# Gate operands laid out in pairs of tokens, and five of layer 0's eight output weight blocks loaded beside the last steps of the recurrence

## The chip, the cores and the metric

The kernel runs on one core of a Trainium2 chip. A core has five engines that run side by side, each through its own instructions in order: TensorE (PE, matmuls; its weight loads are listed apart as PEld), VectorE (DVE), ScalarE (ACT), GpSimd (POOL) and SyncE (SP), which mostly issues DMAs. The metric is the device time of one launch in microseconds.

## The reference

The reference is a trunk of two layers over 256 context tokens and 512 latent tokens of width 1024. Each layer has a mixer and a feed-forward part, both inside a residual with adaLN modulation:

```python
mix, mix_c = mixer(h, hc, *mix_p, need_ctx=not last)
x = x + g1 * mix
x = x + g2 * peer_ffn(rms_norm(x, norm2) * (1.0 + sc2) + sh2, *peer_p)
```

The mixer of layer 0 is a recurrence (RWKV-7 heads, in both directions) beside a two-dimensional Fourier transform; both are joined and multiplied by `w_out`, a matrix of 1024x1024. The mixer of layer 1 is attention beside a convolution. The feed-forward part looks up experts: for each token and each of 8 heads, 16 of 128x128 experts are chosen by top-k, and only their rows of `pu` and `pv` count:

```python
expert = e1 * N_KEYS + e2
gate = jax.nn.softmax(score, axis=-1)
act = jax.nn.gelu(jnp.einsum("thkd,td->thk", pu[expert], tc).astype(jnp.float32),
                  approximate=False) * gate
return jnp.einsum("thk,thkd->td", act.astype(pv.dtype), pv[expert])
```

## The kernel before, in words

Tokens are worked on in tiles of 128: two tiles of context and four of latent tokens. Matrices are split into a high and a low part in a reduced float32 type, and each product is made of three matmuls (high by high, high by low, low by high).

The feed-forward part has two ways of computing the same thing. For some tiles (the two context tiles in layer 0, one latent tile in layer 1) the chosen rows are **gathered**: GpSimd issues an indirect DMA for one chosen row of each token (line 1128, 128 such steps per tile for `pu` and 128 for `pv`), and VectorE multiplies and sums it (line 1133) or adds it, scaled (line 1142). For the other tiles (four in layer 0, three in layer 1) it is **dense**: all 16384 experts are computed for every token (`up_part`, whose matmuls are line 391 with the output `pS`), then multiplied with a gate matrix that is zero for experts that were not chosen, and multiplied with `pv` (lines 1287 and 1316, output `acc`).

`dense_gates` makes that gate matrix, 128x128 for each token. The 128 choices of a token lie on the partitions. For four tokens at a time VectorE makes one-hot rows of both index halves, `o` (line 1106, compares the iota `iob` with the indices `gxe`), and multiplies one of them with the gate values in a high and a low part, `og` (line 1108, `gxg`). Then, for each of the four tokens, two matmuls (line 1114) contract over the 128 choices: the weights are the 128 one-hot columns of the token, the streamed operand its 128 gated columns. ScalarE evicts four tokens at once (line 1116, two instructions) into `gbig`. Since VectorE writes `o` and `og` with the four tokens innermost, a matmul reads its 128 columns with a step of four float16 elements, 8 bytes.

The mixer of layer 0 (`mixer0`) runs its recurrence in 12 steps (`rwkv_step`). The context tiles are done first, and their feed-forward part runs beside steps 4 to 11. After the recurrence `out_norm` multiplies the latent tiles with `w_out` in the order 3, 4, 2, 5 (line 985, matmuls with the output `po`, 48 per tile). `out_k` (from line 941) loads the eight row blocks of `w_out`: each block in two halves of 512 columns into the buffer `woraw` (line 948), then split: ScalarE casts the high part `wohi` (line 378), GpSimd subtracts for the low part `wolo` (line 381). In the kernel before, `out_w` loads all eight blocks, with three `woraw` buffers (`WL[0]`), inside the front of layer 0's dense part, which stands in a block of raised priority.

The order of instructions on each engine is set by a list scheduler when the program is built. It follows the order in the code, except where a part stands under `tc.high_priority(n)`, which moves it ahead. So the order is fixed before the run, and each engine works through its own list, waiting at semaphores.

Of the kernel before, what the change touches and what calls it, by code (L numbers as in the profile page):

```python
# [8 lines left out]
F32 = mybir.dt.float32  # L9
F32R = mybir.dt.float32r  # L10
BF16 = mybir.dt.bfloat16
F16 = mybir.dt.float16
# [3 lines left out]
OP = mybir.AluOpType  # L16
# [14 lines left out]
CQ = 3  # L31
FB = 2
GSC = 32768.0
GW = 4
GQ = 0
NO = 0
NK = 0
WI = 9
WL = [3, 2]
HF = 300  # L40
OL = [[0, 1, 2, 3], []]
# [25 lines left out]
OB = 4  # L67
# [126 lines left out]
class Net:  # L194
# [26 lines left out]
    def setup(self, st):  # L221
# [22 lines left out]
        self.ka1 = ka  # L244
        self.iob = p.tile([128, 128, GW], F16, name="iob")
        nc.vector.tensor_copy(self.iob, self.k("iota")[:, :, None].to_broadcast([128, 128, GW]))
        self.io16 = p.tile([128, 16, 16], BF16, name="io16")
# [204 lines left out]
    def mixer0(self, st, early, xin, xout, xend):  # L452

        tc = self.tc
        with ExitStack() as s1:
            self.mixer0_in(s1, xin)
            with ExitStack() as s2:
# [24 lines left out]
                for i in range(4, NCH):  # L482
                    with tc.high_priority(HP):
                        self.rwkv_step(i)
                    if i == WI and NO + NK == 0:
                        wo = []
                    elif i == WI:
                        wk = self.tp(early, "ow", 1, side="right")
                        wo = self.out_k(wk, 0, range(NK))
                        oe = {t: wk.tile([128, 8, 128], F32, name=f"od{t}") for t in (2, 3, 4, 5)[4 - NO:]}  # L490
# [596 lines left out]
    def dense_gates(self, e1, e2, gate, gd, sp, gp, pp, pt):  # L1087

        nc = self.nc
        V = nc.vector  # L1090


        ee, gg = sp.tile([128, 2, 128], F16, name="gxe"), sp.tile([128, 2, 128], F16, name="gxg")
        for dst, x, sc in ((ee[:, 0], e1, 1.0), (ee[:, 1], e2, 1.0), (gg[:, 0], gate, GSC)):
            p = pt.tile([128, 128], F32, name="gtp")
            nc.tensor.transpose(p, x.rearrange("p a b -> p (a b)"), self.k("ident"))
            nc.scalar.mul(out=dst, in_=p, mul=sc)
        V.scalar_tensor_tensor(out=gg[:, 1], in0=p, scalar=GSC, in1=gg[:, 0], op0=OP.mult, op1=OP.subtract)
        W, H = GW, 64
        for h0 in range(0, 128, H):  # L1100
            gh = [gp.tile([128, 64, H], F32, name="gbig") for _ in range(2)]
            for t0 in range(h0, h0 + H, W):
                w = slice(t0, t0 + W)
                o = sp.tile([128, 2, 128, W], F16, name="o12", bufs=OB)
                og = sp.tile([128, 2, 128, W], F16, name="og", bufs=OB)
                V.tensor_tensor(out=o, in0=self.iob[:, None].to_broadcast([128, 2, 128, W]),  # L1106
                                in1=ee[:, :, None, w].to_broadcast([128, 2, 128, W]), op=OP.is_equal)
                V.tensor_tensor(out=og, in0=o[:, 0:1].to_broadcast([128, 2, 128, W]),  # L1108
                                in1=gg[:, :, None, w].to_broadcast([128, 2, 128, W]), op=OP.mult)
                for k0 in range(0, W, 4):  # L1110
                    p = pp.tile([128, 4, 128], F32, name="gps")
                    for j in range(4):
                        for i in range(2):
                            nc.tensor.matmul(p[:, j, :], o[:, 1, :, k0 + j], og[:, i, :, k0 + j], start=(i == 0), stop=(i == 1))  # L1114
                    for i, g in enumerate(gh):
                        nc.scalar.mul(out=g[:, :, t0 - h0 + k0:t0 - h0 + k0 + 4].rearrange("p e t -> p t e"), in_=p[:, :, i * 64:i * 64 + 64],  # L1116
                                      mul=1.0 / GSC)
            for i, g in enumerate(gh):
                nc.scalar.dma_start(gd[h0 // H, :, i * 64:i * 64 + 64, :], g)

# [500 lines left out]
```

## Time and profile before

| | us |
|---|---|
| median of 3 runs | 4701.33 (4699.65 to 4709.9) |
| the profiled execution | 4686.23 |
| its span, first to last instruction | 4684.4 |
| PE busy | 4278.9 (91%) |
| weight loads of PE busy | 3540.5 (76%) |
| VectorE busy | 3552.1 (76%) |
| ScalarE busy | 1739.0 (37%) |
| GpSimd busy | 1577.4 (34%) |

The mean granted clock of TensorE is 0.95 of full speed (2.4 GHz). Matmuls are pipelined: one starts while the one before it still drains, and its end in the profile is modelled. So the duration of a matmul in the profile is no price; the distance from start to start in an unbroken run is. In the profile's rows a type `f32` on PE can be the reduced type, since both have four bytes; line 391, 985, 1287 and 1316 use the reduced type, lines 558 and 1014 plain float32.

### The profile page before, as it was taken

To read this page: it belongs to the slowest core of one execution; us is meant where nothing else is said; L and a number is where in the kernel's file an instruction comes from. 1 tells how busy PE (TensorE), PEld (TensorE's weight loads), DVE (VectorE), ACT (ScalarE), POOL (GpSimd) and SP (SyncE) were. 2 spreads that over 40 slices of the span, in tenths; PEclk is the share of its full clock that TensorE was granted. 3 is DMA by queue.
4 is the path that set the end of the run, shared out by engine and by line. 5 is a ranking of instruction groups with operands and counts; after the bars stand their busy time and mean duration, and the time that the engine had idled before them with its cause. 6 is when DMAs were issued, how large, how long until landed. Compare 5 with 4: busy or idle time off the path is not lost. (4 is left out here: it accounts for less than half of the span.)

```text
span 4684.4 us, 69766 instructions
## 1 busy us (share of the span) xinstructions
PE 4278.9 (91%) x26113; PEld 3540.5 (76%) x26113; DVE 3552.1 (76%) x6647; ACT 1739.0 (37%) x2845; POOL 1577.4 (34%) x1146
## 2 busy tenths in 40 slices
PE   7998899985769999999999999879999989999998
PEld 5775567874647887877777888666789978888887
DVE  2776566689899887888788787695488877788885
ACT  3443123333224556222222222336436643333333
POOL 1332112214643120444444344383220024444440
PEclk9998898997889999999999999889999989999999
DMA  4444873335777767989888888410135589999994
GB/s 167 97 105 106 268 272 115 111 127 184 225 240 266 250 242 263 321 303 322 292 306 314 302 307 286 154 31 32 70 110 183 201 326 330 337 350 334 335 332 153
DMA packets 487278, 1061.99 MB, mean 227 GB/s; under 512 B 95094, under 2 KB 265846, under 8 KB 477206
## 3 DMA queue, kind: packets, MB, share of 16 engines
q1 hardware_dynamic: 371740, 594.02, 38.5%
q0 software_dynamic: 110592, 402.70, 24.6%
q10 hardware_dynamic: 4608, 60.82, 3.3%
q8 instruction: 205, 3.36, 0.3%
q14 instruction: 133, 1.09, 0.1%
HBM read 927.83 MB, written 129.56 MB: 226 GB/s over the span
## 5 line engine op out<-in xcount | busy, mean ns | idle before, releaser
L1128 POOL DMA_INDIRECT row<-in_l_pv_dram,gi x384 | 539.0, 1404 | 912.1 <-DVE rows L1142 778.1
L1128 POOL DMA_INDIRECT row<-in_l_pur_dram,gi x384 | 477.5, 1243 | 972.2 <-DVE ga L1133 511.7
L391 PE MATMUL pS<-h2hi,whi 128*128 128x512 f32 (+1 forms) x2048 | 754.6, 368 | 36.9 <-ACT a L1233 32.2
L391 PE MATMUL pS<-h2hi,wlo 128*128 128x512 f32 (+1 forms) x2048 | 752.7, 368 | 5.1 <-DVE wlo L381 5.1
L391 PE MATMUL pS<-h2lo,whi 128*128 128x512 f32 (+1 forms) x2048 | 751.8, 367 | 0.0
L1133 DVE CUSTOM_DVE_ANT_0 row<-row,rows 128x1024 f32<-128x1024 f32 x384 | 495.7, 1297 | 170.5 <-DMA row<-in_l_pur_dram,gi 168.1
L378 ACT CAST whi<-wraw 128x1024 fp32r<-128x1024 f32 x327 | 343.9, 1053 | 750.5 <-PE pS L391 571.6
L1142 DVE SCALAR_TENSOR_TENSOR rows<-row,ga,rows 128x1024 f32<-128x1024 f32 x381 | 488.2, 1281 | 158.5 <-DMA row<-in_l_pv_dram,gi 156.4
L1287 PE MATMUL acc<-vhi,ahi 128*128 128x512 f32 x1536 | 469.6, 392 | 11.3 <-ACT ahi L378 11.3
L1287 PE MATMUL acc<-vlo,ahi 128*128 128x512 f32 x1536 | 478.3, 391 | 0.0
L1287 PE MATMUL acc<-vhi,alo 128*128 128x512 f32 x1536 | 472.1, 391 | 3.5 <-DVE alo L381 3.5
L391 PEld LDWEIGHTS pS<-h2hi,whi 128*128 128x128 f32 x2048 | 390.3, 191 | 84.6 <-ACT a L1233 34.1
L391 PEld LDWEIGHTS pS<-h2hi,wlo 128*128 128x128 f32 x2048 | 389.3, 190 | 47.8 <-DVE wlo L381 6.8
L391 PEld LDWEIGHTS pS<-h2lo,whi 128*128 128x128 f32 x2048 | 390.5, 191 | 44.0
L381 DVE TENSOR_TENSOR wlo<-wraw,whi 128x1024 fp32r<-128x1024 f32 x266 | 325.6, 1224 | 85.6 <-ACT whi L378 84.8
L378 ACT CAST vhi<-vraw 128x1024 fp32r<-128x1024 f32 x256 | 265.0, 1050 | 215.3 <-PE acc L1287 107.7
L381 DVE TENSOR_TENSOR vlo<-vraw,vhi 128x1024 fp32r<-128x1024 f32 x256 | 309.8, 1221 | 40.1 <-ACT vhi L378 39.9
L1287 PEld LDWEIGHTS acc<-vhi,alo 128*128 128x128 f32 x1536 | 289.0, 188 | 66.3 <-DVE alo L381 5.1
L1287 PEld LDWEIGHTS acc<-vhi,ahi 128*128 128x128 f32 x1536 | 288.1, 189 | 65.9 <-ACT ahi L378 11.9
L1287 PEld LDWEIGHTS acc<-vlo,ahi 128*128 128x128 f32 x1536 | 289.3, 188 | 61.3
L378 ACT CAST ahi<-a32f 128x384 fp32r<-128x384 f32 (+1 forms) x148 | 83.3, 563 | 594.6 <-DVE a32f L1303 279.5
L1116 ACT ACTIVATE gbig<-gps 128x256 f32<-128x256 f32 x448 | 235.5, 661 | 156.8 <-PE gps L1114 144.4
(460 smaller groups left out, 8175.9 us busy)
## 6 DMA issues: line engine op xcount, KB each, us to landing
wraw<-in_l_pu_dram SPq DMA_DIRECT2D x256, 512.0 KB
vraw<-in_l_pv_dram SPq DMA_DIRECT2D x256, 512.0 KB
gd<-gbig ACTq DMA_DIRECT2D x28, 2048.0 KB
mw<-in_l_mod_w_dram SPq DMA_DIRECT2D x48, 1024.0 KB
gt<-gd SPq DMA_DIRECT2D x64, 512.0 KB
wraw<-in_l_pq_dram SPq DMA_DIRECT2D x48, 512.0 KB
gt<-gd SPq DMA_DIRECT2D x64, 384.0 KB
ab<-arb SPq DMA_DIRECT2D x24, 768.0 KB
```

What stands on the lines that cost most here:

```text
L378: e.copy(out=hi, in_=src)
L381: return (e_lo or nc.vector).tensor_tensor(out=lo, in0=src, in1=hi.bitcast(F32), op=OP.subtract)
L391: nc.tensor.matmul(ps, a[:, k, :], b[:, k, t0:t0 + n], start=s, stop=e)
L1116: nc.scalar.mul(out=g[:, :, t0 - h0 + k0:t0 - h0 + k0 + 4].rearrange("p e t -> p t e"), in_=p[:, :, i * 64:i * 64 + 64], mul=1.0 / GSC)
L1128: nc.gpsimd.indirect_dma_start(out=r, out_offset=None, in_=self.I[f"l{l}_{src}"], in_offset=bass.IndirectOffsetOnAxis(ap=idx[:, s:s + 1], ...
L1133: V.tensor_tensor_reduce(out=r, in0=r, in1=acc, scale=1.0, scalar=0.0, op0=OP.mult, op1=OP.add, accum_out=act[:, s:s + 1])
L1142: V.scalar_tensor_tensor(out=acc, in0=r, scalar=act[:, s:s + 1], in1=acc, op0=OP.mult, op1=OP.add)
L1287: nc.tensor.matmul(acc[t][h2], x[:, q], y[:, h2 * 512:(h2 + 1) * 512], start=s, stop=z)
```

## The change

In `dense_gates` the operands are laid out in pairs of tokens (`GW` 2): a group of four tokens is two pairs, and within a pair the two tokens are innermost. A matmul now reads its columns with a step of two float16 elements, 4 bytes. VectorE still has two instructions for four tokens, each of 1024 elements; the matmuls and the evictions are as many as before, of the same shapes. The small tiles `gxe` and `gxg` are laid out in pairs as well, and the iota has 256 columns in place of 512.

In `mixer0`, after step 8 of the recurrence in the code (`WI` 8), `out_k` is called for row blocks 0 to 4 (`NK` 5) with two `woraw` buffers, outside any raised priority; `out_w` then loads blocks 5 to 7.

```diff
-GW = 4
+GW = 2
-NK = 0
-WI = 9
+NK = 5
+WI = 8
...
-        ee, gg = sp.tile([128, 2, 128], F16, name="gxe"), sp.tile([128, 2, 128], F16, name="gxg")
-        for dst, x, sc in ((ee[:, 0], e1, 1.0), (ee[:, 1], e2, 1.0), (gg[:, 0], gate, GSC)):
+        W, H = GW, 64
+        two = lambda x: x.rearrange("p (a b) -> p a b", b=W)
+        ee, gg = sp.tile([128, 64, 2, W], F16, name="gxe"), sp.tile([128, 64, 2, W], F16, name="gxg")
+        for dst, x, sc in ((ee[:, :, 0], e1, 1.0), (ee[:, :, 1], e2, 1.0), (gg[:, :, 0], gate, GSC)):
...
-            for t0 in range(h0, h0 + H, W):
-                w = slice(t0, t0 + W)
-                o = sp.tile([128, 2, 128, W], F16, name="o12", bufs=OB)
-                og = sp.tile([128, 2, 128, W], F16, name="og", bufs=OB)
...
+            for t0 in range(h0, h0 + H, 4):
+
+                w = slice(t0 // W, t0 // W + 2)
+                o = sp.tile([128, 2, 2, 128, W], F16, name="o12", bufs=OB)
+                og = sp.tile([128, 2, 2, 128, W], F16, name="og", bufs=OB)
+                B4, B5 = [128, 4, 128, W], [128, 2, 2, 128, W]
...
+                V.tensor_tensor(out=og, in0=o[:, :, 0:1].to_broadcast(B5), in1=gg[:, w, :, None].to_broadcast(B5), op=OP.mult)
+                p = pp.tile([128, 4, 128], F32, name="gps")
+                for j in range(4):
+                    a, b = divmod(j, W)
+                    for i in range(2):
+                        nc.tensor.matmul(p[:, j, :], o[:, a, 1, :, b], og[:, a, i, :, b], start=(i == 0), stop=(i == 1))
```

Line numbers in `dense_gates` and `gather` shift by two to three: the row gather is line 1130 after, its multiply line 1135.

The first place where the order moves is GpSimd (POOL) around the output projection of layer 0. `wolo` of block 0 to 7 is numbered 11404, 11414 and so on to 11474 before; after, blocks 0 to 4 are 9860 to 9900, blocks 5 to 7 are 11457 to 11477. `row` is the buffer of a gathered row. Before:

```order
L894 TENSOR_TENSOR hy<-hy,hm 128x768 x2
L381 TENSOR_TENSOR wolo_11404<-woraw,wohi_11403 128x512 x2
L381 TENSOR_TENSOR wolo_11414<-woraw,wohi_11413 128x512 x2
L381 TENSOR_TENSOR wolo_11424<-woraw,wohi_11423 128x512 x2
L381 TENSOR_TENSOR wolo_11434<-woraw,wohi_11433 128x512 x2
L381 TENSOR_TENSOR wolo_11444<-woraw,wohi_11443 128x512 x2
L381 TENSOR_TENSOR wolo_11454<-woraw,wohi_11453 128x512 x2
L1128 DMA row<-in_l_pur_dram,gi_7653 128x1024 x3
L381 TENSOR_TENSOR wolo_11464<-woraw,wohi_11463 128x512 x2
L381 TENSOR_TENSOR wolo_11474<-woraw,wohi_11473 128x512
L1128 DMA row<-in_l_pur_dram,gi_7653 128x1024
L381 TENSOR_TENSOR wolo_11474<-woraw,wohi_11473 128x512
```

After, at the same place:

```order
L381 TENSOR_TENSOR wolo_11457<-woraw,wohi_11456 128x512 x2
L381 TENSOR_TENSOR wolo_11467<-woraw,wohi_11466 128x512 x2
L381 TENSOR_TENSOR wolo_11477<-woraw,wohi_11476 128x512 x2
L894 TENSOR_TENSOR hy<-hy,hm 128x768 x2
L1130 DMA row<-in_l_pur_dram,gi_7653 128x1024 x15
L381 TENSOR_TENSOR wolo_9860<-woraw,wohi_9859 128x512
L1130 DMA row<-in_l_pur_dram,gi_7653 128x1024
L381 TENSOR_TENSOR wolo_9860<-woraw,wohi_9859 128x512
L1130 DMA row<-in_l_pur_dram,gi_7653 128x1024 x2
L381 TENSOR_TENSOR wolo_9870<-woraw,wohi_9869 128x512
L1130 DMA row<-in_l_pur_dram,gi_7653 128x1024
L381 TENSOR_TENSOR wolo_9870<-woraw,wohi_9869 128x512
```

Blocks 5 to 7 now stand ahead of the recurrence's last multiply (`hy`), and blocks 0 to 4 behind it and behind 15 gathers; each further half is followed by one or two gathers, so that 28 stand ahead of the last half of block 4.

The second place is SyncE (SP), which issues the loads: `hsq` and `ot` belong to the end of the recurrence, `wraw` and `sk` to the feed-forward part of the context. Before:

```order
L206 DMA hsq<-yd_121 128x768 x2
L206 DMA sk<-in_l_sk_dram 128x128
L206 DMA wraw<-in_l_pq_dram 128x1024
L206 DMA sk<-in_l_sk_dram 128x128
L206 DMA gr_11401<-modd_84 128x1024
L948 DMA woraw<-in_l_w_out_dram 128x512 x3
L206 DMA ot<-od_7763 128x1024
L206 DMA ox<-in_x_dram 128x1024 x2
L948 DMA woraw<-in_l_w_out_dram 128x512 x3
L206 DMA ot<-od_7764 128x1024
L948 DMA woraw<-in_l_w_out_dram 128x512 x10
```

After:

```order
L206 DMA gr_11454<-modd_84 128x1024
L948 DMA woraw<-in_l_w_out_dram 128x512 x3
L206 DMA hsq<-yd_121 128x768 x2
L206 DMA sk<-in_l_sk_dram 128x128
L206 DMA wraw<-in_l_pq_dram 128x1024
L948 DMA woraw<-in_l_w_out_dram 128x512 x3
L206 DMA sk<-in_l_sk_dram 128x128
L206 DMA ot<-od_7763 128x1024
L206 DMA ox<-in_x_dram 128x1024 x2
L206 DMA ot<-od_7764 128x1024
L948 DMA woraw<-in_l_w_out_dram 128x512 x10
```

The six halves of blocks 5 to 7 have moved up, ahead of `hsq` and `ot`; the ten halves of blocks 0 to 4 stand where the last ten stood. The third place is PE at the start of the projection; after:

```order
L909 MATMUL sm<-xg,g_3801 128x128 x3
L985 MATMUL po<-wohi_9859,oh 128x512 x4
L985 MATMUL po<-wolo_9860,oh 128x512
L985 MATMUL po<-wohi_9859,ol 128x512
L985 MATMUL po<-wolo_9860,oh 128x512 x2
L985 MATMUL po<-wohi_9859,ol 128x512
L985 MATMUL po<-wolo_9860,oh 128x512
L985 MATMUL po<-wohi_9869,oh 128x512 x2
```

As before, the projection begins with block 0; the blocks that are ready first, 5 to 7, are the last that a tile needs.

## Rows read from the trace of the kernel before

**Rows 1.** The page: span, busy time, PE in tenths of 40 slices.

```profile
span 4684.4 us, 69766 instructions
...
PE 4278.9 (91%) x26113; PEld 3540.5 (76%) x26113; DVE 3552.1 (76%) x6647; ACT 1739.0 (37%) x2845; POOL 1577.4 (34%) x1146
...
PE   7998899985769999999999999879999989999998
```

**Rows 2.** All engines in three stretches; columns: window, length, busy time (instructions), clock, DMA.

```profile
core 0: us, PE busy (x) PEld busy (x) DVE busy (x) ACT busy (x) POOL busy (x), PEclk, DMA share, GB/s
1488.00:1810.00 322.00, 322.00 (x1797) 270.87 (x1797) 271.28 (x511) 182.49 (x303) 56.11 (x40) 1.00 0.69 244
1810.00:1900.00 90.00, 80.59 (x449) 66.25 (x447) 66.42 (x90) 51.08 (x87) 17.69 (x10) 0.89 0.76 279
3494.00:3790.00 296.00, 288.33 (x1895) 276.85 (x1894) 250.59 (x570) 192.20 (x317) 5.99 (x5) 0.98 0.55 200
```

**Rows 3.** Line 1114: duration min/median/max in ns, and who waited for it.

```profile
L1114 PEld LDWEIGHTS <-o x1792: 111/117/138, 1488.1 to 3789.5; 128*128 128x128 f16 x200
L1114 PE MATMUL gps<-og,o x1792: 273/297/303, 1488.1 to 3789.6; 128*128 128x128 f16 x200
...
  DVE o L1106: 52.3, 66
```

**Rows 4.** Line 1114 alone in the two gate stretches.

```profile
1488.00:1810.00 322.00, 103.23 (x792) 85.82 (x792) 1.00 0.69 244
3494.00:3790.00 296.00, 100.95 (x768) 82.86 (x768) 0.98 0.55 200
```

**Rows 5.** Timeline of PE: start, duration, line, operands, shape, count.

```profile
1488.12 2.98 PE L1114 MATMUL gps<-og,o 128*128 128x128 f16 x24
...
1491.41 0.39 PE L391 MATMUL pS<-h2hi,wlo 128*128 128x512 f32 x1
1491.64 0.39 PE L391 MATMUL pS<-h2hi,whi 128*128 128x512 f32 x1
```

**Rows 6.** Timeline of PE in the projection: 256 columns streamed.

```profile
130.58 0.28 PE L391 MATMUL pjc<-h0hi,whi 128*128 128x256 f32 x1
...
131.53 0.28 PE L391 MATMUL pjc<-h0hi,wlo 128*128 128x256 f32 x1
```

**Rows 7.** Timeline of PE: float32 products with 2 columns streamed.

```profile
432.80 0.70 PE L558 MATMUL pg<-kt,ib 128*128 128x2 f32 x5
```

**Rows 8.** Timeline of PE: float32 products with 128 columns streamed.

```profile
1212.84 1.06 PE L1014 MATMUL psc<-sk,q 128*128 128x128 f32 x8
```

**Rows 9.** Line 558: durations.

```profile
L558 PE MATMUL pg<-kt,ib x72: 165/251/251, 120.5 to 433.2; 128*128 128x2 f32 x72
```

**Rows 10.** Groups of VectorE: busy us, mean ns, idle before and its releasers.

```profile
L381 DVE TENSOR_TENSOR wlo<-wraw,whi 128x1024 fp32r<-128x1024 f32 x266 | 325.6, 1224 | 85.6 <-ACT whi L378 84.8
...
L1106 DVE TENSOR_TENSOR o<-iob,gxe 128x1024 f16<-128x1024 f16 x224 | 151.9, 687 | 54.0 <-PE gps L1114 52.3 <-issue 0.7 <-ACT gxe L1097 0.3
L1108 DVE TENSOR_TENSOR og<-o,gxg 128x1024 f16<-128x1024 f16 x224 | 148.1, 683 | 0.1
```

**Rows 11.** All engines from the output projection to the first gate.

```profile
1100.00:1490.00 390.00, 279.63 (x1200) 222.78 (x1199) 346.87 (x1040) 95.18 (x139) 197.86 (x153) 0.85 0.76 245
```

**Rows 12.** Groups of VectorE from 1000 to 1490 us.

```profile
L1133 DVE CUSTOM_DVE_ANT_0 row<-row,rows 128x1024 f32<-128x1024 f32 x122 | 177.0, 1456 | 38.8 <-DMA row<-in_l_pur_dram,gi 38.6
```

**Rows 13.** Timeline of POOL around the output projection.

```profile
1103.42 1.15 POOL L1128 DMA_INDIRECT row<-in_l_pur_dram,gi  x1 [2.71 <-DVE tci L1027]
...
1118.70 1.42 POOL L381 TENSOR_TENSOR wolo<-woraw,wohi 128x512 fp32r<-128x512 f32 x1
...
1148.03 1.15 POOL L1128 DMA_INDIRECT row<-in_l_pur_dram,gi  x1 [2.92 <-DVE ga L1133]
```

**Rows 14.** Line 985, the output projection, in two stretches.

```profile
1083.00:1148.00 65.00, 33.16 (x96) 20.79 (x95) 0.71 0.54 175
1148.00:1184.00 36.00, 22.18 (x88) 17.44 (x87) 0.93 0.72 240
```

More of the change, by code (lines that the diff above doesn't have):

```diff
@@ L1095, in dense_gates @@
             p = pt.tile([128, 128], F32, name="gtp")
             nc.tensor.transpose(p, x.rearrange("p a b -> p (a b)"), self.k("ident"))
-            nc.scalar.mul(out=dst, in_=p, mul=sc)
-        V.scalar_tensor_tensor(out=gg[:, 1], in0=p, scalar=GSC, in1=gg[:, 0], op0=OP.mult, op1=OP.subtract)
-        W, H = GW, 64
+            nc.scalar.mul(out=dst, in_=two(p), mul=sc)
+        V.scalar_tensor_tensor(out=gg[:, :, 1], in0=two(p), scalar=GSC, in1=gg[:, :, 0], op0=OP.mult, op1=OP.subtract)
         for h0 in range(0, 128, H):
@@ L1101, in dense_gates @@
             gh = [gp.tile([128, 64, H], F32, name="gbig") for _ in range(2)]
-            for t0 in range(h0, h0 + H, W):
-                w = slice(t0, t0 + W)
-                o = sp.tile([128, 2, 128, W], F16, name="o12", bufs=OB)
-                og = sp.tile([128, 2, 128, W], F16, name="og", bufs=OB)
[L1106 to L1117, printed above, removed]
@@ new lines, in dense_gates @@
+            for t0 in range(h0, h0 + H, 4):
[3 more added lines that the diff above has]
+                B4, B5 = [128, 4, 128, W], [128, 2, 2, 128, W]
+                V.tensor_tensor(out=o.rearrange("p a h e b -> p (a h) e b"), in0=self.iob[:, None].to_broadcast(B4),
+                                in1=ee[:, w].rearrange("p a h b -> p (a h) b")[:, :, None].to_broadcast(B4), op=OP.is_equal)
+                V.tensor_tensor(out=og, in0=o[:, :, 0:1].to_broadcast(B5), in1=gg[:, w, :, None].to_broadcast(B5), op=OP.mult)
[4 more added lines that the diff above has]
+                        nc.tensor.matmul(p[:, j, :], o[:, a, 1, :, b], og[:, a, i, :, b], start=(i == 0), stop=(i == 1))
+                for i, g in enumerate(gh):
+                    nc.scalar.mul(out=g[:, :, t0 - h0:t0 - h0 + 4].rearrange("p e t -> p t e"), in_=p[:, :, i * 64:i * 64 + 64],
+                                  mul=1.0 / GSC)
```

## The prediction

> **What bounds the kernel now.** I read the page first: TensorE (PE) is busy for 4278.9 of 4684.4 us, and in its row of slices it is at 9 in slices 15 to 28 and again from slice 32 on [rows 1]. A microsecond taken from PE can therefore be a microsecond of the run, where no other engine is close behind. Next I cut out the stretches in which the gates are built. From 1488 to 1810 us (layer 0) PE is busy for all of 322 us at clock 1.00, VectorE (DVE) for 271.28; from 3494 to 3790 us (layer 1) PE for 288.33 of 296 us, DVE for 250.59 [rows 2]. So PE sets the time there, and DVE stands some 45 to 50 us behind it. VectorE even waits 52.3 us for line 1114 to hand back an operand buffer [rows 3]. ScalarE (182.49 and 192.20 us) and the transfers (0.69 and 0.55 of the DMA engines) are not near a limit [rows 2].
>
> Of what PE does there I took line 1114 by itself: 792 of its 1792 matmuls lie in the first stretch, 768 in the second [rows 4], and 232 more between 1810 and 1900 us (1024 for layer 0's four tiles of 256). The busy time that rows 4 give (103.23 us) is not its price, as the ends of overlapped matmuls are modelled. The price is the distance between starts: 24 of them take 2.98 us, the last 0.297 of it [rows 3, 5], so (2.98 - 0.297) / 23 = 0.117 us each, 1792 x 0.117 = 210 us of PE.
>
> **Part one, the operands' step.** Each of these matmuls loads 128 columns of weights and streams 128 columns, both float16, and takes its columns out of a tile in which neighbours are 4 tokens apart, 8 bytes. After the change they are 2 tokens apart, 4 bytes. What would it cost then? The trace has no float16 matmul with a 4-byte step, so I bound it by rows of 4-byte elements that lie side by side. Neighbouring starts of a 512-column matmul are 0.23 us apart (1491.41, 1491.64) [rows 5]; eight intervals of 256 columns take 131.53 - 130.58 = 0.95 us, 0.119 each [rows 6]. That is 256 / 2.4 = 107 ns of streaming at one column per cycle, and 12 ns beside it. The gate matmul of 128 columns costs as much as one of 256: its step of 8 bytes fits a column every second cycle. By the same line 128 columns at full rate cost 53 + 12 = 65 ns. Eight float32 products of 128 columns take 1.06 us, 0.112 each if the last takes 0.28 [rows 8]; that is 2 x 128 / 2.4 and 5 ns, so two passes over the columns, 0.056 for one. So the lower bound is 0.056, the upper 0.117 (no gain; a dearer one nothing suggests, as the array does the same work). I take 0.065, as its row is the nearest in kind: one pass. Saving: 53 ns per matmul, 42 us in the first stretch, 12 between 1810 and 1900, 41 in the second.
>
> The Trainium skill ("TensorE: Matmul & The Clock Gate", section "Back-to-back issue gap") gives 81 ns for a sustained pair of weight load and matmul at 128 columns; an estimate by that page's figure would be a saving of 36 ns, 28 + 8 + 28 us. No run here shows an 81.
>
> Not all of it can be kept. In the first stretch PE falls to 322 - 42 = 280 us while DVE keeps 271; in the second to 247.6 while DVE keeps 250.6 [rows 2]. DVE does as many instructions on as many elements as before. Two engines so even, coupled through a few buffers, lose some: I take 36 of 42, 30 of 41 and, where PE is busy only 80.59 of 90 us [rows 2], 4 of 12. Sum: 70 us. What follows (the up and down products) keeps PE at 9 and more [rows 1], so it starts earlier and ends earlier by that much.
>
> For DVE the same layout has a price that the trace does not show: the broadcast operand of lines 1106 and 1108 has runs of 2 elements, 4 bytes, where it had 4. Bounds: 0.68 us for 1024 elements as now, or 1.22 us, the price of 1024 float32 elements [rows 10]; below 0.68 it cannot go by the layout, as the count of elements is the same. I take 0.68, since the row is of the same operation and type and the innermost run is still longer than one. The casts that fill the small tiles in pairs (three per token tile) and the iota of half the size are a few instructions of 128 columns per tile, under 1 us together in either direction.
>
> **Part two, the output weights.** The order shows that five blocks are not early. They are not raised in priority, and the three blocks of out_w are; SyncE issues the three first, and blocks 0 to 4 come last, through two raw buffers in place of three. POOL's splits of them stand behind 15 row gathers, and the last behind 28; in the kernel before 4 stood ahead of the last split. The projection needs block 0 first, so it waits. Queued behind POOL's splits are the gathers, behind PE's first projection matmul the other three row tiles and the h2 norms.
>
> Price: the first gather starts at 1103.42 us, the last split at 1118.70; 15 gathers start in the 44.6 us up to 1148.03, 3.2 us each [rows 13]. After, 28 of them stand ahead of the last split: at 3.2 us it ends near 1103 + 90 = 1193, and at the 1.456 us that DVE needs for one [rows 12] near 1103 + 41 + 10 splits of 1.4 = 1158. So the last split is 40 to 74 us late. PE then has all but the first matmuls of 192 left: at 0.23 us 44 us. The projection's end moves from 1184 [rows 14] to 1202 to 1237, 18 to 53 us later. That is covered: DVE sets the pace from 1100 to 1490 us, with 346.87 of 390 us busy, PE 279.63 [rows 11], and the gathers' multiplies that it does in the meantime are ones it would do anyway (244 before the first gate in both orders). What is not covered is DVE's waiting for gathered rows, now 38.6 us for 122 [rows 12], as it has less else to do: I take 5 us, between -15 (rows waited for less later on) and +40 (most of the delay is uncovered).
>
> **Sum.** -70 + 5 = -65 us: 4686.23 profiled (1.83 of it around the span) becomes 4621. The median of the runs is 15.1 us above the profiled one, so 4701.33 - 65 = 4636 us.
>
> **Rivals.**
> - *The pair stays at 0.117.* A weight load with 128 columns would then set the distance, not the step. For it: 5 float32 products that load 128 columns and stream only 2 take 0.70 us, the last 0.251, thus 0.112 each [rows 7, 9], close to 0.117; if their load is one pass, a load costs what a gate pair costs. Against it: if it is two passes, as their streaming is, a load is 0.056, and the pair of rows 8 at the same 0.112 says the same of both. The time: 4701 + 5 = 4706, with part two's ends 4686 to 4741. Chance 0.18. A rule that leads here too: the Trainium skill ("SBUF — State Buffer", section "Door 1: The DMA port swizzle (why `[64,N]` ≈ `[32,N]`)") has lines of 16 bytes and full bandwidth from two hits per line, and a step of 8 bytes already has two. By that rule the step is free now; rows 5 and 6, where 128 columns cost like 256, rather speak against it, without settling it.
> - *A part comes back.* The gain is there, but DVE and the hand-offs keep half of part one, or the late projection is uncovered: -35 + 5 = -30 at half, or -70 + 40 = -30. For it: DVE's 250.59 us against PE's remaining 247.6. Against: the 52.3 us for which DVE waits for PE now. 4671 us, chance 0.20.
> - *Slower: VectorE falls to one element per cycle.* Place: lines 1106 and 1108, 448 instructions, +0.54 us each. In the first stretch 198 of them lie beside the 792 matmuls (two for every 8): DVE 271 + 107 = 378 us against 322, in the second 192: 251 + 104 = 355 against 296, and 58 in the 90 us: +31 on 66.42, 8 over. It would cost 56 + 59 + 8 + 5 = 128 us: 4829. It decides once an instruction costs over (322 - 271) / 198 = 0.26 us more than 0.68; below that PE's gain covers it. Chance 0.05.
>
> **How the numbers follow.** Forecast 0.57, with a range of its own of 4606 to 4666; the three rivals 0.18, 0.20, 0.05. At the low end the whole saving (95 us) and -15 from part two give 4591, at the high end the first rival with 15 us from part two 4716; I take 4592 to 4716. Within 0.2% (9.4 us, about what can be told from no change): 0.10 of the first rival, 0.03 of the second, 0.13 in all. Faster: 0.57 + 0.15 + 0.02 = 0.74. Slower: 0.05 + 0.02 + 0.06 = 0.13.
>
> **What would show it.** Runs of gate matmuls at about 0.065 us between starts; PE below 100% in the gate stretches and VectorE above 90%, its instructions still at 0.68 us, and its wait for line 1114 mostly gone; the first gate matmul within 10 us of 1488; the last split of wolo between 1158 and 1193 us. Wrong it would be by gate matmuls still at 0.117, by VectorE at 1.2 us per instruction, or by a first gate that comes 20 us late.

## The result and the profile after

The changed kernel takes 4651.28 us (median of 4 runs, 4637.62 to 4672.79), the kernel before 4700.49 in the runs beside it: a ratio of 0.9899, with a 95% interval of 0.9857 to 0.9941. That is 49 us less, where 65 were forecast. Its profiled execution takes 4651.99 us.

The page has PE at 4192.2 us, 87 less than before [rows 1], and the span only 34 us shorter (the profiled execution before, 4686.23 us, lay 14 us below the median of its kernel):

```profile
span 4650.2 us, 69814 instructions
...
PE 4192.2 (90%) x26113; PEld 3453.7 (74%) x26113; DVE 3539.1 (76%) x6647; ACT 1732.4 (37%) x2845; POOL 1610.3 (35%) x1146
...
PE   7998899982677999989999999888999989999998
```

A run of gate matmuls on PE (start, duration, line, operands, count) and the line's durations in ns, with the wait of VectorE for it:

```profile
1503.17 1.55 PE L1116 MATMUL gps<-og,o 128*128 128x128 f16 x24
```

```profile
L1116 PEld LDWEIGHTS <-o x1792: 96/97/146, 1503.2 to 3757.7; 128*128 128x128 f16 x200
L1116 PE MATMUL gps<-og,o x1792: 217/218/308, 1503.2 to 3757.8; 128*128 128x128 f16 x200
...
  DVE o L1109: 12.2, 13
```

(1.55 - 0.218) / 23 = 0.058 us from start to start, against 0.117 [rows 3, 5]: at these distances 1792 x 0.059 = 106 us of PE are gone. VectorE's wait for operand buffers falls from 52.3 us to 12.2. All engines over the gate stretches of both layers, from the first gate matmul to the last (window, length, busy time of PE, weight loads, VectorE, ScalarE, GpSimd, then clock and DMA share), before and then after, and VectorE's two instructions (busy us, mean ns):

```profile
1488.00:1850.00 362.00, 355.40 (x2043) 298.81 (x2043) 304.95 (x565) 215.33 (x366) 56.11 (x40) 0.97 0.67 239
3532.00:3790.00 258.00, 251.65 (x1684) 240.55 (x1683) 213.92 (x451) 169.65 (x289) 5.99 (x5) 0.97 0.56 206
```

```profile
1503.00:1831.00 328.00, 328.00 (x2189) 268.80 (x2187) 303.94 (x558) 218.56 (x373) 74.65 (x40) 1.00 0.75 272
3531.00:3758.00 227.00, 212.15 (x1679) 201.46 (x1677) 209.69 (x450) 166.07 (x286) 7.66 (x6) 0.97 0.65 235
```

```profile
L1111 DVE TENSOR_TENSOR og<-o,gxg 128x1024 f16<-128x1024 f16 x224 | 147.6, 686 | 0.1
L1109 DVE TENSOR_TENSOR o<-iob,gxe 128x1024 f16<-128x1024 f16 x224 | 147.4, 686 | 13.4 <-PE gps L1116 12.2 <-ACT gxe L1099 0.7
```

Layer 0's gates now lie within 328 us and layer 1's within 227, where the matmuls' first and last starts were 361 and 257 us apart before. In layer 0 PE is now busy for all of 328.00 us. VectorE's price is unchanged at 686 ns [rows 10].

Around the output projection the trace has GpSimd's first gather, first late split and last split:

```profile
1104.11 1.14 POOL L1130 DMA_INDIRECT row<-in_l_pur_dram,gi  x1 [39.59 <-DVE tci L1027]
...
1140.08 1.27 POOL L381 TENSOR_TENSOR wolo<-woraw,wohi 128x512 fp32r<-128x512 f32 x1
...
1176.13 1.28 POOL L381 TENSOR_TENSOR wolo<-woraw,wohi 128x512 fp32r<-128x512 f32 x1
```

The last split comes at 1176.13 us, 57 us later than before [rows 13]. The last matmuls of the projection, before and then after:

```profile
1172.59 0.39 PE L985 MATMUL po<-wohi,ol 128*128 128x512 f32 x1
```

```profile
1229.45 0.39 PE L985 MATMUL po<-wohi,ol 128*128 128x512 f32 x1
```

So the projection ends 57 us later too. PE's longest waits from 1080 to 1300 us (waiting line, what it waited for, sum, times, longest) are for these blocks:

```profile
PE po L985 <- ACT wohi L378: 51.2, 6, 43.3
PE po L985 <- POOL wolo L381: 34.7, 8, 25.2
```

From 1100 to 1490 us PE is busy 247.15 us in place of 279.63, VectorE 329.01 in place of 346.87 [rows 11], and VectorE's wait for gathered rows (at the end of its row) is 56.9 us in place of 38.8 [rows 12]:

```profile
1100.00:1490.00 390.00, 247.15 (x1022) 192.44 (x1023) 329.01 (x1002) 82.31 (x121) 206.09 (x158) 0.78 0.72 232
```

```profile
L1135 DVE CUSTOM_DVE_ANT_0 row<-row,rows 128x1024 f32<-128x1024 f32 x122 | 179.5, 1476 | 56.9 <-DMA row<-in_l_pur_dram,gi 56.3
```

The products `pS` of the up weights that PE has done before the first gate matmul (1488 us before, 1503 after; PE's busy time and count stand behind the length) are fewer. Before, then after:

```profile
1000.00:1488.00 488.00, 111.00 (x432) 87.90 (x432) 9.93 (x17) 0.85 0.70 226
```

```profile
1000.00:1503.00 503.00, 76.84 (x286) 59.81 (x286) 6.42 (x11) 0.79 0.66 212
```

146 products at 0.23 us (33 us of PE) had been done ahead of the gates and now stand between them (2189 matmuls in layer 0's gate stretch for 2043), and the gates begin 15 us later: 48 us that the gates' gain has to pay first. Not all of the 15 need come from the change: in the eight traces with all blocks in `out_w` the first gate matmul starts between 1482 and 1501 us, in the four with five blocks in `out_k` between 1503 and 1512.

### The profile page after: what moved, and what is told of

Read it like the earlier page. It is cut to its first block, busy times and chain, and to the rows that moved or that the text cites. A ratio compares the mean times of both kernels' runs of the same rounds, so it can differ in the third digit from the quotient of the medians.

```text
span 4650.2 us, 69814 instructions
## 1 busy us (share of the span) xinstructions
PE 4192.2 (90%) x26113; PEld 3453.7 (74%) x26113; DVE 3539.1 (76%) x6647; ACT 1732.4 (37%) x2845; POOL 1610.3 (35%) x1146
## 3 DMA queue, kind: packets, MB, share of 16 engines
q1 hardware_dynamic: 371740, 594.02, 38.8%
## 5 line engine op out<-in xcount | busy, mean ns | idle before, releaser
L1130 POOL DMA_INDIRECT row<-in_l_pv_dram,gi x384 | 559.9, 1458 | 830.6 <-DVE rows L1144 696.2
L1130 POOL DMA_INDIRECT row<-in_l_pur_dram,gi x384 | 487.4, 1269 | 1011.4 <-DVE ga L1135 576.6
L1289 PE MATMUL acc<-vhi,ahi 128*128 128x512 f32 x1536 | 471.1, 392 | 12.2 <-ACT ahi L378 10.3
```

The source lines that it names most:

```text
L1130: nc.gpsimd.indirect_dma_start(out=r, out_offset=None, in_=self.I[f"l{l}_{src}"], in_offset=bass.IndirectOffsetOnAxis(ap=idx[:, s:s + 1], ...
L1289: nc.tensor.matmul(acc[t][h2], x[:, q], y[:, h2 * 512:(h2 + 1) * 512], start=s, stop=z)
```

## Experiments

### Each part alone

```diff
 # e1: the pairs only
-NK = 5
-WI = 8
+NK = 0
+WI = 9
```

> Only the pair layout of the gate operands; all eight blocks of the output weights are loaded as before. Theory A (the early blocks cost layer 0 what the gates give it, by the late output projection and VectorE's longer waiting for gathered rows): the first gate matmul back near 1488 us, the end of layer 0's dense part some 35 to 45 us earlier than in the changed kernel, the whole 4605 to 4625 us. Theory B (the early blocks are covered, and layer 0 gives the gates' gain back after 1840 us because row gathers and transfers pace that stretch): layer 0's dense part ends where it ends in the changed kernel, the whole 4640 to 4660 us.

```diff
 # e2: the early blocks only, in the kernel before
-NK = 0
-WI = 9
+NK = 5
+WI = 8
```

> Only the five blocks in out_k, the gate operands as in the kernel before. Theory A: the last split of wolo near 1176 us, the projection's end 45 us late, the whole 25 to 45 us slower than the kernel before (4725 to 4745 us). Theory B: the projection as late, but the whole within 10 us of the kernel before.

Pairs alone: 4619.62 us against 4696.59, ratio 0.9837 (0.9811 to 0.9862). Blocks alone: 4742.9 us, ratio 1.0097 (1.0073 to 1.0121). So the first part brings 77 us and the second takes 46; their sum, -31, lies within the interval of the changed kernel. Theory A fits both times, B neither; of its details, layer 0's dense part ends 27 us earlier with pairs alone than in the changed kernel (at 2953.7 us for 2980.4), not 35 to 45. On top of the pairs the same blocks cost less, 32 us (4651.28 - 4619.62), though the intervals overlap. The products before the first gate matmul, pairs alone and then blocks alone (same columns, up to the first gate matmul of each):

```profile
1000.00:1494.00 494.00, 110.59 (x432) 86.76 (x432) 9.93 (x17) 0.83 0.69 224
```

```profile
1000.00:1508.00 508.00, 77.06 (x286) 59.62 (x286) 6.42 (x11) 0.79 0.65 211
```

432 with all blocks in `out_w`, 286 with five in `out_k`, whatever the gates' layout. PE's head start goes with the second part alone, and so does VectorE's wait for gathered rows from 1000 to 1490 us: 38.6 us with pairs alone, 56.7 with blocks alone.

### Which operand's step

```diff
 # e4a, on e1: weights o four tokens apart, streamed og in pairs
-o = sp.tile([128, 2, 2, 128, W], F16, name="o12", bufs=OB)
+o = sp.tile([128, 2, 128, 4], F16, name="o12", bufs=OB)
...
-nc.tensor.matmul(p[:, j, :], o[:, a, 1, :, b], og[:, a, i, :, b], ...)
+nc.tensor.matmul(p[:, j, :], o[:, 1, :, j], og[:, a, i, :, b], ...)
 # e4b, on e1: weights in pairs, streamed og four tokens apart
-og = sp.tile([128, 2, 2, 128, W], F16, name="og", bufs=OB)
+og = sp.tile([128, 2, 128, 4], F16, name="og", bufs=OB)
...
-nc.tensor.matmul(p[:, j, :], o[:, a, 1, :, b], og[:, a, i, :, b], ...)
+nc.tensor.matmul(p[:, j, :], o[:, a, 1, :, b], og[:, i, :, j], ...)
 # e5, on the kernel before: groups of eight
-GW = 4
+GW = 8
-OB = 4
+OB = 2
```

> Blocks as in the kernel before; only the streamed operand og in pairs (4 bytes from column to column), the weights o four tokens apart (8 bytes); og is made by two VectorE instructions of 512 elements. If the streamed operand's step alone set the distance: starts 0.057 us apart. If the weights' step set it, or either at 8 bytes is enough to hold it: 0.117 us. If a weight load and the stream share one read path: about 0.09 us.

> The opposite: the weights o in pairs (4 bytes), the streamed operand og four tokens apart (8 bytes). If the streamed operand's step sets the distance: 0.117 us as in the kernel before. If the weights' step sets it: 0.057. If both share one read path: about 0.09 us.

> The kernel before with groups of eight tokens (a step of 16 bytes; two buffers for the operands in place of four, as they are twice as large). If each doubling of the step doubles the streaming: 128 x 4 / 2.4 + 12 = 0.225 us between starts, some 190 us of PE more. If any step over 4 bytes costs the same: 0.117 us, and within 20 us of the kernel before.

With only the streamed operand in pairs, the one run took 4615.86 us; with only the weights in pairs 4688.88; with eights 4979.8. The matmul runs, in that order, each with the durations of its line:

```profile
1501.26 0.66 PE L1118 MATMUL gps<-og,o 128*128 128x128 f16 x8
```

```profile
L1118 PEld LDWEIGHTS <-o x1792: 111/113/149, 1484.5 to 3720.6; 128*128 128x128 f16 x200
L1118 PE MATMUL gps<-og,o x1792: 217/221/312, 1484.5 to 3720.7; 128*128 128x128 f16 x200
```

```profile
1501.36 1.09 PE L1116 MATMUL gps<-og,o 128*128 128x128 f16 x8
```

```profile
L1116 PE MATMUL gps<-og,o x1792: 273/296/301, 1482.3 to 3793.8; 128*128 128x128 f16 x200
```

```profile
1512.10 3.93 PE L1114 MATMUL gps<-og,o 128*128 128x128 f16 x16
```

```profile
L1114 PEld LDWEIGHTS <-o x1792: 142/146/173, 1492.8 to 4080.9; 128*128 128x128 f16 x200
L1114 PE MATMUL gps<-og,o x1792: 387/413/449, 1492.8 to 4081.1; 128*128 128x128 f16 x200
```

(0.66 - 0.221) / 7 = 0.063 us; (1.09 - 0.296) / 7 = 0.113 in the second; (3.93 - 0.413) / 15 = 0.234 in the third. The streamed operand's step sets the price, and doubling the step of both operands doubles it: 4, 8 and 16 bytes cost 0.058, 0.117 and 0.234. Weights 8 bytes apart load in 113 ns in place of 97; at 0.063 us from start to start they cost at most 5 ns a matmul, and the time of that run shows nothing of it. The eights lost more than forecast: 288 us (4979.8 against 4691.55), where some 190 us of PE were expected. The distance explains 1792 x 0.117 = 210 of them; the two operand buffers in place of four changed as well, and what the rest is due to was not tested.

### Why the blocks come late

```diff
 # e3: raised priority
-wo = self.out_k(wk, 0, range(NK))
+with tc.high_priority(1500):
+    wo = self.out_k(wk, 0, range(NK))
 # e7: the early ones are the last that the projection needs
-wo = self.out_k(wk, 0, range(NK))
+wo = self.out_k(wk, 0, range(8 - NK, 8))
...
-return [*ws, *self.out_k(wp, l, range(len(ws), 8), WL[l])], gr
+return [*self.out_k(wp, l, range(8 - len(ws)), WL[l]), *ws], gr
```

> The changed kernel, with the five early blocks under the same raised priority as the other three. Theory P (their order comes from the missing priority, as the prediction says): blocks 0 to 4 split before the last recurrence step, the projection back near 1184 us, about 4610 us. Theory S (their buffers lie where the context tiles' selection keeps its buffers until about 1113 us): the last split again near 1176 us, 4635 to 4670 us.

> The changed kernel, but the five blocks in out_k are 3 to 7 and out_w loads 0 to 2, so that the projection begins with blocks that are there. If PE's waiting for block 0 is what costs: 4615 to 4630 us. If the last block's lateness decides (28 gathers stand ahead of its split as before): 4640 to 4660 us, the projection's end again near 1230 us.

Raised, the one run took 4657.62 us, with the last split where it was or later:

```profile
1184.59 1.28 POOL L381 TENSOR_TENSOR wolo<-woraw,wohi 128x512 fp32r<-128x512 f32 x1
```

The order on PE, VectorE, ScalarE and GpSimd is the same as without the raise, so theory P falls. That their buffers stand in the way fits: the pool `ow` is opened on the side of the buffers from which the context tiles' route and selection have just been closed in the code, while on the chip the selection's last copy on ScalarE (line 1075) starts at 1111.57 us and takes 1.90, and the casts of block 0 follow it at 1113.38; VectorE's part of the selection goes on until 1135. A pool in another place was not tried, so the place is argued, not shown. Nor was a third `woraw` buffer: the cast of the third late half waits 30.70 us for its load, until 1145.21, and with two buffers that load can only come once the first late split (1140.08) is done.

With blocks 0 to 2 split early (until 1057 us) and 3 to 7 late, the last split stays late:

```profile
1051.96 5.60 POOL L381 TENSOR_TENSOR wolo<-woraw,wohi 128x512 fp32r<-128x512 f32 x3 [1.83 <-DMA woraw<-in_l_w_out_dram]
...
1178.73 1.28 POOL L381 TENSOR_TENSOR wolo<-woraw,wohi 128x512 fp32r<-128x512 f32 x1
```

4645.35 us, ratio 0.9885 (0.9863 to 0.9908): next to nothing of the 46 us comes back. The last block decides when the projection ends (1230 us, as before the swap), not the first.

### What keeps the rest of the gates' gain

By the distance between starts, pairs alone save 106 us of PE. Its busy time on the page falls by 75 (to 4203.8 us), the time of the kernel by 77. I took VectorE for the next limit.

```diff
 # e6, on e1: GpSimd makes some low parts (GB: 10 blocks of layer 0, 12 of layer 1)
-*u, i = self.wtile(up, self.I[f"l{l}_pu"][b], e_lo=V, q=nc.sync)
+*u, i = self.wtile(up, self.I[f"l{l}_pu"][b], e_lo=G if b in GB[l] else V, q=nc.sync)
 # e8, on e1: these low parts are left out, the high part stands in for them
-            return hi, lo, self.split(raw, hi, lo, None, e_lo)
+            return (hi, hi, self.nc.scalar.copy(out=hi, in_=raw)) if skip else (hi, lo, self.split(raw, hi, lo, None, e_lo))
 # e9, on e1: layer 0's gathers start later beside the up blocks
-PACE = [(60, 0.5, 0.25, 3), (48, 0.5, 0.5, 3)]
+PACE = [(60, 0.5, 0.25, 2), (48, 0.5, 0.5, 3)]
```

> Pairs only (as e1), and GpSimd makes the low part of 10 up weight blocks of layer 0 and 12 of layer 1, which fall beside the gates, in place of VectorE (22 x 1.22 = 27 us off VectorE). If VectorE is what limits the gate stretches now: 4600 to 4612 us, the stretches shorter by 5 to 12 us each. If the hand-offs between the engines limit them: 4615 to 4625. If GpSimd's slower split comes late for PE: over 4625.

> Pairs only (as e1), without the low part of 10 up weight blocks of layer 0 and 12 of layer 1 that fall beside the gates (their high part is used in its place, so the matmuls are as many): 22 x 1.22 = 27 us off VectorE and nothing put in its place. If VectorE is what keeps the gates' gain at 77 us in place of the matmuls' 107: 4594 to 4606 us, the gate stretches shorter by 5 to 13 us each. If the hand-offs between the engines keep it: within 8 us of e1's 4620.

> Pairs only (as e1), layer 0's row gathers spread from the middle of the up blocks that are paced instead of their first third, so that fewer of VectorE's additions of gathered rows (1.28 us each) fall beside the gates. If VectorE limits the gate stretch and the later stretch has room: layer 0's gates end 10 to 30 us earlier and the whole at 4595 to 4612 us. If the later stretch (transfers at 0.88) has no room: the gates end earlier, but the dense part of layer 0 where it did, 4615 to 4630 us or more.

On GpSimd: 4650.25 us, ratio 0.9892 (0.9868 to 0.9916), 30 us worse than pairs alone. GpSimd's split and VectorE's multiply and additions from 1490 to 1900 us (busy us, mean ns, idle before):

```profile
L382 POOL TENSOR_TENSOR wlo<-wraw,whi 128x1024 fp32r<-128x1024 f32 x10 | 34.2, 3423 | 133.6 <-ACT whi L379 133.6
```

```profile
L1112 DVE TENSOR_TENSOR og<-o,gxg 128x1024 f16<-128x1024 f16 x128 | 92.4, 745 | 0.2
...
L1145 DVE SCALAR_TENSOR_TENSOR rows<-row,ga,rows 128x1024 f32<-128x1024 f32 x54 | 77.5, 1435 | 12.1 <-DMA row<-in_l_pv_dram,gi 12.0
```

A split takes 3.4 us there, and VectorE's instructions beside it slow down: 745 ns in place of 683 for the gate multiply, 1435 in place of 1279 for the addition. That run can't tell what VectorE's load costs. Leaving the low parts out can: 4626.35 us, ratio 0.9858 (0.9827 to 0.9888), no faster than pairs alone. All engines in the gate stretches, pairs alone and then without the low parts:

```profile
1490.00:1820.00 330.00, 314.46 (x2086) 256.30 (x2085) 305.28 (x574) 214.24 (x368) 78.30 (x41) 0.97 0.76 274
3502.00:3726.00 224.00, 211.30 (x1682) 201.92 (x1682) 209.93 (x450) 166.08 (x289) 5.61 (x5) 0.98 0.65 237
```

```profile
1490.00:1820.00 330.00, 316.43 (x2094) 257.51 (x2092) 291.03 (x556) 215.50 (x370) 65.36 (x40) 0.97 0.77 279
3502.00:3726.00 224.00, 213.36 (x1662) 203.38 (x1660) 200.57 (x439) 163.71 (x282) 18.21 (x15) 0.98 0.71 260
```

VectorE has 14.25 us less to do in the first stretch and 9.36 in the second, and PE gets no more done worth telling (2094 matmuls for 2086, 1662 for 1682). First and last gate matmul lie 313 and 221 us apart there, 317 and 223 with pairs alone: 4 and 2 us closer, where 5 to 13 each were expected. So VectorE's load is not what keeps most of the gain. With later gathers: 4625.08 us, ratio 0.9846 (0.9821 to 0.987), no change either; layer 0's gates end 3 us earlier (10 to 30 were expected) and its dense part where it did.

What is missing is not lost after layer 0's gates. All engines between the gates' end and the end of layer 0's last products, before, with pairs alone, and with only the weights in pairs, where the gates gain nothing:

```profile
1850.00:2978.00 1128.00, 1082.90 (x4692) 880.91 (x4693) 884.95 (x1061) 305.73 (x401) 467.54 (x349) 0.99 0.88 303
```

```profile
1811.00:2950.00 1139.00, 1090.71 (x4695) 885.24 (x4695) 885.25 (x1061) 306.03 (x402) 466.53 (x349) 0.99 0.87 300
```

```profile
1843.00:2984.00 1141.00, 1088.92 (x4693) 883.40 (x4692) 885.19 (x1061) 305.32 (x400) 470.77 (x349) 0.99 0.87 299
```

The same number of matmuls (4692, 4695 and 4693) takes 1139 us with pairs alone in place of 1128, but 1141 with only the weights in pairs: the 11 us are not shown to come from the faster gates. 17 us of layer 0's and 12 of layer 1's saving were lost within the gate stretches themselves (317 and 224 us between the first and last gate matmul with pairs alone), and 17 + 12 = 29 is all that is missing from 106. The end of layer 0's gates shows where a part goes. All engines with pairs alone, up to 1770 us and from there on:

```profile
1494.00:1770.00 276.00, 275.42 (x1767) 224.88 (x1767) 263.84 (x507) 178.79 (x300) 77.08 (x40) 1.00 0.78 277
1770.00:1811.00 41.00, 27.62 (x276) 22.50 (x274) 36.24 (x58) 32.55 (x65) 0.00 (x0) 0.78 0.61 237
```

PE has no pauses in the first 276 us and 13 us of them in the last 41, where it waits for `og` of VectorE and for ScalarE's evictions, and where the clock falls to 0.78. Over both stretches PE is idle for 27 us with pairs alone (317 and 224 us, 303.04 and 211.30 of them busy) and for 13 before: about half of the 29. What makes up the rest was not tested; a part is the gate matmuls at the lower clock (last section), which gain little from the pairs. Most of the 29 is not VectorE's load, by the run without low parts.

## Why the prediction was right or wrong

**The operands' step.** Right in direction and cause: the streamed operand at 8 bytes took as long as twice the columns at 4. ("A column every second cycle" holds at 2.4 GHz only: at the lower clock the price at 8 bytes stays what it was, as the last section shows.) The size was a little small, 53 ns forecast and 59 measured, as the 12 ns beside the streaming, taken from products of four-byte elements, are 5 here. The lower bound (a pass of a float32 product, 0.056) was nearer than the value taken.

**The first rival** (the pair stays at 0.117) is out. Its argument from the rows with 2 streamed columns needed their weight load to be one pass; the gate matmuls now start every 0.058 us with weights of 128 columns, so a float16 load of 128 columns does not hold the starts further apart than that. The rule of the Trainium skill that led there ("SBUF — State Buffer", section "Door 1: The DMA port swizzle (why `[64,N]` ≈ `[32,N]`)"), lines of 16 bytes at full bandwidth from two hits on, would have made a step of 8 bytes free; for the streamed operand the runs contradict it, 0.117 us against 0.058.

**What is kept of it.** 70 of 95 us were forecast, 77 of 106 measured: the share came out, but by luck. The reason given, VectorE next behind PE, was not borne out: with 24 us of its work gone nothing was gained. Nor did PE fall below 100% in layer 0's gate stretch, one of the signs asked for: the late products filled it (328.00 of 328 us), with VectorE at 93%. Two readings were off on the way without moving the sum. PE is at 9 in slices 13 to 25, 28 to 32 and 34 to 39 of [rows 1], not "15 to 28 and again from slice 32 on"; and layer 1's gates begin at 3532 us, not 3494, so that VectorE has 213.92 us to do there beside PE's 251.65. VectorE's own price stayed at 0.68 us, so the slower rival is out.

**The early blocks.** The order was read rightly: the last split was forecast between 1158 and 1193 us and came at 1176, the projection's end between 1202 and 1237 and came at 1230. The delay was larger than the forecast 18 to 53 us, 57, since the 1184 it was counted from is only the end of a window of [rows 14]; the projection before ended at 1173. The step that failed is the price: "That is covered: DVE sets the pace from 1100 to 1490 us". +5 us was taken, within -15 to +40, and 46 (34 to 57) was measured. VectorE was the busier engine there, but in the pauses of the order PE did up products ahead of the gates, and these count: PE is the limit in the gate stretch, so a product that is not done by then costs time there. That is the 33 us; the 15 to 20 us by which the gates begin later are the rest. That VectorE's longer waits for rows (18 us) are behind these fits, but was not tested by itself. With the pairs the blocks cost 32 rather than 46; that fits PE's 14 idle us in layer 0's gate stretch with pairs alone, which the late products fill. The first gate at 1503 us, 15 late, lies outside the 10 us that the prediction allowed. The second rival spoke of it as "the late projection is uncovered" and priced it at 40.

**The reason for their lateness** was given as missing priority. Raising it left the order on PE, VectorE, ScalarE and GpSimd as it was.

**The sum.** -65 forecast, -49 measured (28 to 67): the first part brought 7 us more than forecast and the second cost 41 more, which gives -31; the changed kernel's median lies 18 us from that, within the intervals of the three. That the time fell inside the forecast's own 4606 to 4666 us is partly luck: an error of 41 us in the second term was met by 7 in the first and by the 18 in which the parts do not add up.

## What to carry to other kernels

A matmul with few columns is worth a look at its distance from start to start: if it costs as much as one of twice the columns, look at the step of the streamed operand: of the steps tried here with float16 (4, 8 and 16 bytes), 4 bytes cost half of 8; the weights matter less. Before calling a delay covered because another engine is busier in that stretch, ask what the bottleneck of the whole run did in its idle time there: work that it did ahead has to be done later, here for 32 to 46 us. The best version measured here is the pair layout alone, at 4620 us. A raised priority alone did not make the early load early here; that it needs a place for its buffers that is free early is argued, not shown.

## What the runs showed of the hardware that was not expected

The weights' step hardly matters: 8 bytes from column to column cost 113 ns per load in place of 97, with the matmuls 0.063 us apart. A step of 16 bytes in both operands still follows the doubling, with 0.234 us, and the loads then take 146 ns:

```
step of both operands, bytes   us between starts   weight load, ns (median)
4                              0.058               97
8                              0.117               117
16                             0.234               146
```

These prices are those at the full granted clock. At 0.50, the lower of the two levels (1.2 GHz), only the 4-byte step gets dearer. The line's busy time with the clock (last but two) and a run of gate matmuls in it, for steps of 4 (pairs alone), 8 (before) and 16 bytes (eights):

```profile
1797.00:1803.00 6.00, 5.20 (x48) 4.92 (x47) 0.50 0.74 309
1797.80 5.36 PE L1116 MATMUL gps<-og,o 128*128 128x128 f16 x48 [4.05 <-ACT gbig L1118]
```

```profile
3784.00:3789.90 5.90, 3.88 (x29) 2.83 (x27) 0.50 0.88 312
3787.01 1.10 PE L1114 MATMUL gps<-og,o 128*128 128x128 f16 x8 [1.25 <-DVE og L1108]
```

```profile
1976.00:2016.00 40.00, 33.97 (x145) 20.64 (x144) 0.50 0.25 105
2003.58 15.13 PE L1114 MATMUL gps<-og,o 128*128 128x128 f16 x64 [2.46 <-DVE og L1108]
```

(5.36 - 0.308) / 47 = 0.107 us at 4 bytes (128 columns at 1.2 GHz), (1.10 - 0.297) / 7 = 0.115 at 8 and (15.13 - 0.413) / 63 = 0.234 at 16. So at the lower clock the pairs gain hardly anything, and the price of the wider steps does not follow TensorE's clock.

And a subtraction of 128x1024 float32 elements on GpSimd beside VectorE's gate work took 3.4 us, where the same instruction took 2.4 us on average in the run with pairs alone, and VectorE's multiply beside it took 9% longer.
